# A PEER decoder layer on one core: 170 gathered tokens for 160, and gate pieces of 38 tokens for 32

## The chip, the cores and the metric

The kernel runs on one core of a Trainium2 chip. The metric is the device time of one execution in microseconds (us). The kernel before was run three times, and the median counts. The traces come from the hardware profiler, of one execution each.

## What is computed

The reference is one decoder layer over 512 tokens of width 2048, all in float32: modulation from a conditioning vector, a projection with a short convolution and a differential attention, an output projection, and then the PEER feed-forward part, on which the change works:

```python
def peer_ffn(h, w_q, keys1, keys2, expert_u, expert_v):   # 8 heads, 128 x 128 experts
    ...                                                   # idx, g: (T, 8, 16), the 16 best experts of each head
        u = jnp.take(expert_u, ib, axis=0)
        a = jnp.einsum('thkd,td->thk', u, xb)
        w = (jax.nn.gelu(a.astype(jnp.float32), approximate=False) * gb).astype(xb.dtype)
        vv = jnp.take(expert_v, ib, axis=0)
        return jnp.einsum('thk,thkd->td', w, vv)
```

Each token picks 128 of the 16,384 experts. An expert is a row of `expert_u` and a row of `expert_v`, 2048 floats (8 KB) each.

## The kernel before

The first third of the kernel computes the layer up to the queries of the experts. Then it treats the tokens in two ways, side by side.

**Dense tokens** (`TD = T - TG`, the last 352). All 128 blocks of 128 experts are multiplied with all of these tokens. `u_block(e)` loads block e of `expert_u` (`ur`), turns it on VectorE where it was laid out for that (`u_turn`, `transpose`), and splits it into a high and a low part (`split`: ScalarE makes the high part, VectorE subtracts and writes the low part, both into `ut`). TensorE then does 48 matmuls (16 chunks of the width, three products of high and low parts) with TD columns into `pa`, and ScalarE applies gelu into `ge`. `w_block` multiplies by the gates `g4` and splits the product into `W`. `v_group(ch, dg)` does the same with `expert_v`: for each chunk `ch` of 8 blocks and each quarter `dg` of the width it loads, splits (`vs`) and multiplies, 96 matmuls with TD columns, and VectorE adds the result to `acc`. There are 16 chunks. `ut` and `vs` have two buffers each.

**The gate stage** comes before: for each dense token a 128 x 128 table of gates is made by one matmul of two one-hot tables (`oh` made on VectorE, `og` on GpSimd and ScalarE, eight tokens at a time), and stored to `g_dram` in pieces of `GB` tokens.

**Gathered tokens** (the first `TG` = 160). One token lies on each partition, and an indirect DMA of GpSimd fetches for each partition the row of one of its experts, 1 MB in all (`gathered`, tile `gt`, three buffers). VectorE multiplies it with the token and sums (`gather_u`), and later adds the row of `expert_v` times its weight to `gacc` (`gather_v`). The first 128 tokens take 128 gathers of u and 128 of v. The other 32 tokens form a second group: they lie four times over the partitions (`fold` = 4), each copy taking 32 of a token's 128 experts, so 32 gathers of u and 32 of v. `gather_next` brings the second group's tokens, indices and gates to their places.

`gather_to` spreads these steps evenly over the blocks of the dense part, up to the end of chunk 14. At the end `begin`, `add_gathered` and `store` add everything up for each quarter `dg`: `add_gathered` turns `gacc` on TensorE and sums the copies of the second group on VectorE.

The order of the instructions on each engine is set by a scheduler that works from its own model of times. It keeps the dependences, and each engine then runs its own list strictly in order. So a vector operation that waits for a gather holds up the splits behind it, and TensorE waits for the splits.

Of the kernel before, what the change touches and what calls it, by code (L numbers as in the profile page):

```python
# [15 lines left out]
AF = mybir.ActivationFunctionType  # L16
OP = mybir.AluOpType
# [5 lines left out]
P = 128  # L23
# [8 lines left out]
THETA = 10000.0  # L32
LAM_INIT = 0.8 - 0.6 * math.exp(0.0)

TG = 160
TD = T - TG
CH = 8
AHEAD = 1
GB = 32
GBUF = 3  # L40
LAG = 3
PASSES = ((0, 0), (0, 1), (1, 0))
# [16 lines left out]
OG_ACT = 2  # L59
# [20 lines left out]
def hymba_peer(tc, x, c, positions, w_ada, b_ada, norm1_g, w_in, conv_w, q_norm_g, k_norm_g,  # L80
               lambda_q1, lambda_k1, lambda_q2, lambda_k2, subln_g, w_out, norm2_g,
               w_peer_q, sub_keys1, sub_keys2, expert_u, expert_v, out):
    nc = tc.nc
    x, out = x[0], out[0]
# [14 lines left out]
    with ExitStack() as ctx:  # L99
        const = ctx.enter_context(tc.tile_pool(name="const", bufs=1))  # L100
        y_dram = tc.dram_tile([KC, P, T], F32, name="y_dram")
        x1_dram = tc.dram_tile([KC, P, T], F32, name="x1_dram")
        g_dram = tc.dram_tile([TD // GB, NK, NK, GB], F32, name="g_dram")
        u_dram = tc.dram_tile([NK, P, D], F32, name="u_dram")
        h_dram = tc.dram_tile([TG - P, D], F32, name="h_dram")
        a_dram = tc.dram_tile([P, D], F32, name="a_dram")
# [29 lines left out]
        def px():  # L136
            return psX.tile([P, T], F32, name="px")
# [521 lines left out]
        gate = [(res if i < NG else tk).tile([P, P], F32, name=f"gate{i}", bufs=1) for i in range(NT)]  # L659
# [3 lines left out]
        def dense_tokens(n, behind):  # L663
            k, r = divmod(n, 4)
            q, m = divmod(k, 4)
            t = nc.scalar.activation(hd[4 * m + r][q * 32:(q + 1) * 32],
                                     h2T[k][r * 32:(r + 1) * 32, :, TG:].bitcast(F32), AF.Copy)
            tc.add_manual_dep(t.ins, behind.ins.name, ORDER, reason="work left for the weights")
# [93 lines left out]
        idxu = [None] * NT  # L762
        opT = [None] * NT
        if NG == 2:
            w = P // fold
            ib = res.tile([P, w], U32, name="ib")
            gb_ = res.tile([P, w], F32, name="gb_")

        def finish_select(i):
            gv = gate[i].rearrange("p (h k) -> p h k", k=16)  # L770
# [89 lines left out]
        def w_block(e):  # L860
            if e % 4 == 0:
                G4[0] = up.tile([P, TD // GB, 4, GB], F32, name="g4", bufs=1)
                nc.sync.dma_start(G4[0], g_dram[:, :, e:e + 4, :].rearrange("b p i t -> p b i t"))
            if e % 2 == 0:
                return
            ge = GE.pop(e // 2)
            g_ = ge.rearrange("p i (b t) -> p i b t", t=GB)
            nc.vector.tensor_tensor(out=g_, in0=g_, in1=G4[0][:, :, e % 4 - 1:e % 4 + 1, :].rearrange("p b i t -> p i b t"),
# [42 lines left out]

        def gather_next():
            nc.sync.dma_start(a_dram, gacc)
            w = P // fold
            for f in range(fold):
                nc.sync.dma_start(h2n[f * nb:(f + 1) * nb, :], h_dram)
                nc.sync.dma_start(ib[f * nb:(f + 1) * nb, :], idxu[1][0:nb, f * w:(f + 1) * w])
                nc.sync.dma_start(gb_[f * nb:(f + 1) * nb, :], gate[1][0:nb, f * w:(f + 1) * w])

        steps = []  # L920
        for g in range(NG):
            w = P if g == 0 else P // fold
            if g:
                steps.append((gather_next, ()))
            steps += [(gather_u, (g, j)) for j in range(w)] + [(gather_w, (g, w))] + [(gather_v, (g, j)) for j in range(w)]
# [25 lines left out]
        with tc.tile_pool(name="gs", bufs=2, side="right") as gs:  # L951
            ios = gs.tile([P, P], F32, name="ios", bufs=1)
            nc.gpsimd.iota(ios, pattern=[[1, P]], base=0, channel_multiplier=0, allow_small_or_imprecise_dtypes=True)
            iof = psI.tile([P, P], F32, name="iof")
            nc.scalar.activation(iof, ios, AF.Copy)
            nb_ = TD // GB
            for b in range(nb_):
                gt_ = gs.tile([P, NK, GB], F32, name="gtile")
                for t8 in range(0, GB, 8):
                    i, tt = divmod(TG + b * GB + t8, P)  # L960
                    o = opT[i]
                    oh = gp.tile([P, D], F32, name="gt", bufs=GBUF).rearrange("p (a t n) -> p a t n", a=2, n=P)
                    nc.vector.tensor_tensor(out=oh, in0=iof[:, None, None, :].to_broadcast([P, 2, 8, P]),  # L963
                                            in1=o[:, 0:2, tt:tt + 8, None].to_broadcast([P, 2, 8, P]), op=OP.is_equal)
                    og = gs.tile([P, 8, P], F32, name="og", bufs=OG_BUFS)
                    m = 8 - OG_ACT
                    nc.gpsimd.tensor_tensor(out=og[:, 0:m], in0=oh[:, 0, 0:m],
                                            in1=o[:, 2, tt:tt + m, None].to_broadcast([P, m, P]), op=OP.mult)
                    for j in range(m, 8):
                        nc.scalar.activation(og[:, j], oh[:, 0, j], AF.Copy, scale=o[:, 2, tt + j:tt + j + 1])  # L970
                    for t4 in (4, 0):
                        pg = psV.tile([P, 4, P], F32, name="pv")
                        for j in range(4):
                            gm = nc.tensor.matmul(pg[:, j], oh[:, 1, t4 + j], og[:, t4 + j], start=True, stop=True)  # L974
                        nc.scalar.activation(gt_[:, :, t8 + t4:t8 + t4 + 4], pg.rearrange("p t n -> p n t"), AF.Copy)
                nc.sync.dma_start(g_dram[b], gt_)
                lay_out(min(1 + (b % 8 == 7), len(lay)), gm)
                if b >= nb_ - (RUN - NT):
                    u_block(RUN - nb_ + b, behind=gm if b == nb_ - 1 else None)

# [133 lines left out]
```

## Time and profile before

| what | value |
|---|---|
| time, median of 3 runs | 3346.73 us (3344.19 to 3349.19) |
| the profiled execution: its own time | 3349.88 us |
| its span, first to last instruction | 3347.6 us |
| TensorE busy | 95% of the span |
| VectorE busy | 82% of the span |
| mean granted TensorE clock | 0.978 of 2.4 GHz |

The shares are means over stages with different limits. The profile's time axis starts at the first instruction; the gate stage lies at about 1255 to 1400 us, the dense part with its gathers at 1400 to 3256 us, and the end behind it. In a window's row, an engine's busy time counts operations that overlap once, whereas a group's busy time adds up the durations.

### The profile page before, as it was taken

The numbers are of one execution on the slowest core, as the hardware profiler recorded it, in microseconds if no ns is written. First come the engines' busy times: TensorE is split into PE (matmuls) and PEld (weight loads), VectorE is DVE, ScalarE is ACT, GpSimd is POOL, SyncE is SP. The second block draws the span as 40 slices with busy tenths as digits, with TensorE's granted clock in tenths as the row PEclk, the third lists the DMA queues.
The fourth block names the chain that finished last, engine by engine and source line by source line (L and its number), as shares of the span: only waits on it lengthen the run. The fifth ranks groups of instructions, "written<-read, shape, count | busy, mean of one in ns | idle before, by whom it ended". The sixth has DMA issues, their size and how long they took to land.

```text
span 3347.6 us, 47029 instructions
## 1 busy us (share of the span) xinstructions
PE 3176.0 (95%) x18006; PEld 2945.2 (88%) x18006; DVE 2739.1 (82%) x3631; ACT 1223.3 (37%) x1866; POOL 1057.7 (32%) x709
## 2 busy tenths in 40 slices
PE   5889999999999859999999999999999999999998
PEld 4777877777777659999999999999999999999997
DVE  6888477842338998789999899999999999999975
ACT  5246343343255336632333333333333333333322
POOL 2447333353435634312222232222222222222210
PEclk9999999999999979999999999999999999999998
DMA  9878978966979878989989899998988898999964
GB/s 303 283 257 294 345 250 280 299 211 221 315 256 302 261 243 288 335 290 364 343 332 343 310 333 363 325 338 323 340 333 316 336 354 329 360 330 338 338 222 158
DMA packets 388896, 1017.81 MB, mean 304 GB/s; under 512 B 29713, under 2 KB 108478, under 8 KB 328126
## 3 DMA queue, kind: packets, MB, share of 16 engines
q1 hardware_dynamic: 342590, 679.23, 59.8%
q0 software_dynamic: 46080, 335.56, 25.7%
q8 instruction: 141, 2.31, 0.3%
q14 instruction: 85, 0.70, 0.1%
HBM read 965.11 MB, written 171.18 MB: 339 GB/s over the span
## 4 chain that ended last, share of the span: by engine, by line
PE 55%; DVE 4%; issue 2%; DMA 1%; ACT 0%; POOL 0%; DVEq 0%; ACTq 0%; SPq 0%; POOLq 0%
PE pa L835 26%; PE pv L1004 26%; PE pv L974 2%; DVE gacc L910 1%; DVE ut L90 1%; DMA xs<-x_dram 1%; DVE gt L963 1%; DVE ur L823 1%; DVE vs L90 1%; DMA gt<-in_expert_v_dram,idxu 0%; DMA gt<-in_expert_u_dram,idxu 0%; ACT ut L89 0%; DVE acc L1020 0%; PE pv L1061 0%; DVE gt L897 0%
## 5 line engine op out<-in xcount | busy, mean ns | idle before, releaser
L835 PE MATMUL pa<-hd,ut 128*128 128x352 f32 x6144 | 1067.2, 326 | 37.5 <-DVE ut L90 23.6
L1004 PE MATMUL pv<-W,vs 128*128 128x352 f32 x6144 | 1052.1, 325 | 5.1 <-ACT W L89 2.6
L835 PEld LDWEIGHTS pa<-hd,ut 128*128 128x128 f32 x6144 | 1010.9, 190 | 42.4 <-DVE ut L90 26.6
L1004 PEld LDWEIGHTS pv<-W,vs 128*128 128x128 f32 x6144 | 1001.8, 189 | 8.0 <-ACT W L89 3.5
L90 POOL TENSOR_TENSOR wsp<-wraw,wsp 128x1024 fp32r<-128x1024 f32 x160 | 389.0, 2434 | 557.6 <-ACT wsp L89 525.4
L89 ACT ACTIVATE vs<-vr 128x1024 fp32r<-128x1024 f32 x256 | 271.6, 1061 | 737.9 <-PE pv L1004 687.8
L89 ACT ACTIVATE ut<-ur 128x1024 fp32r<-128x1024 f32 x256 | 269.6, 1056 | 315.2 <-PE pa L835 239.5
L897 DVE SCALAR_TENSOR_TENSOR gt<-gt,h2n 128x2048 f32<-128x2048 f32 x160 | 364.6, 2283 | 18.3 <-DMA gt<-in_expert_u_dram,idxu 18.3
L910 DVE SCALAR_TENSOR_TENSOR gacc<-gt,ga_a,gacc 128x2048 f32<-128x2048 f32 x158 | 369.9, 2341 | 6.8 <-DMA gt<-in_expert_v_dram,idxu 6.7
L889 POOL DMA_INDIRECT gt<-in_expert_u_dram,idxu x128 | 183.0, 1430 | 554.6 <-DVE gt L897 320.8
L90 DVE TENSOR_TENSOR vs<-vr,vs 128x1024 fp32r<-128x1024 f32 x256 | 311.2, 1216 | 57.3 <-ACT vs L89 56.9
L90 DVE TENSOR_TENSOR ut<-ur,ut 128x1024 fp32r<-128x1024 f32 x256 | 310.9, 1219 | 55.6 <-ACT ut L89 54.4
L889 POOL DMA_INDIRECT gt<-in_expert_v_dram,idxu x128 | 172.4, 1347 | 552.3 <-DVE gacc L910 360.1
L89 ACT ACTIVATE wsp<-wraw 128x1024 fp32r<-128x1024 f32 x160 | 169.2, 1058 | 346.5 <-issue 72.0
L507 PE MATMUL pm<-big,wsp 128*128 128x512 f32 x1152 | 285.2, 401 | 0.0
L823 DVE STREAM_TRANSPOSE ur<-ur 128x1024 f32<-128x1024 f32 x232 | 274.5, 1221 | 0.1
L507 PEld LDWEIGHTS pm<-big,wsp 128*128 128x128 f32 x1152 | 214.9, 191 | 42.6
L282 PE MATMUL pqk<-wsp,big 128*128 128x512 f32 x768 | 190.1, 407 | 18.0 <-DVE qk L334 13.6
L748 PE MATMUL pm<-big,wsp 128*128 128x512 f32 x768 | 188.5, 403 | 19.0 <-POOL wsp L90 17.4
L282 PEld LDWEIGHTS pqk<-wsp,big 128*128 128x128 f32 x768 | 148.7, 196 | 53.0 <-DVE qk L334 17.0
L748 PEld LDWEIGHTS pm<-big,wsp 128*128 128x128 f32 x768 | 147.2, 195 | 52.2 <-POOL wsp L90 20.0
L593 PE MATMUL pm<-big,wsp 128*128 128x512 f32 x768 | 182.1, 397 | 6.2 <-DVE x L599 6.2
(274 smaller groups left out, 3024.0 us busy)
## 6 DMA issues: line engine op xcount, KB each, us to landing
ur<-u_dram SPq DMA_DIRECT2D x128, 1024.0 KB, 7.8
vr<-in_expert_v_dram SPq DMA_DIRECT2D x256, 512.0 KB, 7.2
u_dram<-in_expert_u_dram SPq DMA_DIRECT2D x464, 256.0 KB, 6.7
ada_w<-in_w_ada_dram SPq DMA_DIRECT2D x192, 512.0 KB, 5.5
wraw<-in_w_in_dram SPq DMA_DIRECT2D x96, 512.0 KB, 5.7
g_dram<-gtile SPq DMA_DIRECT2D x11, 2048.0 KB, 7.4
g<-g_dram SPq DMA_DIRECT2D x32, 704.0 KB, 9.4
wraw<-in_w_out_dram SPq DMA_DIRECT2D x32, 512.0 KB, 5.5
```

What stands on the lines that cost most here:

```text
L89: hi = nc.scalar.activation(dst[:, 0], src, AF.Copy)
L90: (eng or nc.vector).tensor_tensor(out=dst[:, 1], in0=src, in1=dst[:, 0].bitcast(F32), op=OP.subtract)
L282: nc.tensor.matmul(banks[i], hT[kk][:, a, i * P:(i + 1) * P], ws[:, b, k], start=(kk == last[0] and n == 0), stop=(kk == last[1] and n == 2))
L507: nc.tensor.matmul(banks[n2], ws[:, a, k, n2 * P:(n2 + 1) * P], hT[kk][:, b], start=(kk == 0 and n == 0), stop=(kk == KC - 1 and n == 2))
L593: nc.tensor.matmul(banks[j], ws[:, a, k, j * P:(j + 1) * P], yT[kk0 + k][:, b], start=(kq == 0 and k == 0 and n == 0), stop=(kq == 7 and k ...
L748: nc.tensor.matmul(banks[j], ws[:, a, k, j * P:(j + 1) * P], h2T[kk][:, b], start=(kk == 0 and n == 0), stop=(kk == KC - 1 and n == 2))
L823: nc.vector.transpose(t, t)
L835: mm = nc.tensor.matmul(pa[:, :TD], ut[:, a, j].rearrange("p b r -> p (b r)"), hd[k][:, b], start=(k == 0 and n == 0), stop=(k == KC - 1 a ...
L889: d = nc.gpsimd.indirect_dma_start(out=t, out_offset=None, in_=src, in_offset=bass.IndirectOffsetOnAxis(ap=gidx[g][:, j:j + 1], axis=0))
L897: return lambda: nc.vector.scalar_tensor_tensor(t, t, 1.0, h2n, op0=OP.mult, op1=OP.mult, accum_out=ga_a[:, j:j + 1])
L910: return lambda: nc.vector.scalar_tensor_tensor(gacc, t, a, gacc, op0=OP.mult, op1=OP.add)
L1004: mm = nc.tensor.matmul(pv[j // 2][:, j % 2, :TD], vs[:, a, bb, j * P:(j + 1) * P], W[e0 // 2][:, m, bb], start=(b == 0 and n == 0), stop= ...
```

## The change

`TG` becomes 170, so 342 tokens are dense, and 42 form the second gathered group. They lie three times over the partitions (126 of 128 used), each copy taking up to 43 of a token's 128 experts; the tables of indices and gates are set to zero first, so that what isn't filled adds nothing. The second group so takes 43 gathers of u and 43 of v where it took 32 and 32. `GB` becomes 38, which makes nine pieces of the 342 tokens. A piece is no multiple of eight, so its last step has six tokens, and a step also ends where the table of 128 tokens ends.

```diff
-TG = 160
+TG = 170
...
-GB = 32
+GB = 38
...
-            w = P // fold
+            w = -(-P // fold)
             ib = res.tile([P, w], U32, name="ib")
             gb_ = res.tile([P, w], F32, name="gb_")
+            nc.vector.memset(ib, 0)
+            nc.vector.memset(gb_, 0.0)
...
             nc.sync.dma_start(a_dram, gacc)
-            w = P // fold
+            w = -(-P // fold)
             for f in range(fold):
+                n = min(w, P - f * w)
                 nc.sync.dma_start(h2n[f * nb:(f + 1) * nb, :], h_dram)
-                nc.sync.dma_start(ib[f * nb:(f + 1) * nb, :], idxu[1][0:nb, f * w:(f + 1) * w])
+                nc.sync.dma_start(ib[f * nb:(f + 1) * nb, 0:n], idxu[1][0:nb, f * w:f * w + n])
...
-            w = P if g == 0 else P // fold
+            w = P if g == 0 else -(-P // fold)
...
-                for t8 in range(0, GB, 8):
-                    i, tt = divmod(TG + b * GB + t8, P)
+                pos = 0
+                while pos < GB:
+                    i, tt = divmod(TG + b * GB + pos, P)
+                    n = min(8, GB - pos, P - tt)
...
-                lay_out(min(1 + (b % 8 == 7), len(lay)), gm)
+                lay_out(min(1 + (b % 3 == 2), len(lay)), gm)
```

The scheduler makes a new order. Two places of it follow. The change moves its line numbers by up to eight: L910 is L912, L868 is L870, L1031 is L1039, L1047 is L1055.

The first is VectorE's list around the last split of a block of `expert_u` (the last row with `ut` on the left). `gacc` rows are the uses of gathered rows of `expert_v`, `xs` rows belong to the end of the kernel. Before:

```order
L910 SCALAR_TENSOR_TENSOR gacc<-gt,ga_a,gacc 128x2048
L868 TENSOR_TENSOR ge<-ge,g_27186 128x704
L90 TENSOR_TENSOR ut<-ur,ut 128x1024
L90 TENSOR_TENSOR vs<-vr,vs 128x1024
L90 TENSOR_TENSOR W<-ge,W 128x704
L90 TENSOR_TENSOR ut<-ur,ut 128x1024
L90 TENSOR_TENSOR vs<-vr,vs 128x1024
L90 TENSOR_TENSOR ut<-ur,ut 128x1024
L868 TENSOR_TENSOR ge<-ge,g_27186 128x704
L90 TENSOR_TENSOR W<-ge,W 128x704
L90 TENSOR_TENSOR vs<-vr,vs 128x1024
L1031 SCALAR_TENSOR_TENSOR xs<-acc,modc,xs 128x352 x4
```

Now, from the last split of `ut` on:

```order
L90 TENSOR_TENSOR ut<-ur,ut 128x1024
L912 SCALAR_TENSOR_TENSOR gacc<-gt,ga_a,gacc 128x2048 x2
L90 TENSOR_TENSOR vs<-vr,vs 128x1024
L912 SCALAR_TENSOR_TENSOR gacc<-gt,ga_a,gacc 128x2048
L870 TENSOR_TENSOR ge<-ge,g_27252 128x684
L912 SCALAR_TENSOR_TENSOR gacc<-gt,ga_a,gacc 128x2048
L90 TENSOR_TENSOR W<-ge,W 128x684
L912 SCALAR_TENSOR_TENSOR gacc<-gt,ga_a,gacc 128x2048 x3
L90 TENSOR_TENSOR vs<-vr,vs 128x1024
L1039 SCALAR_TENSOR_TENSOR xs<-acc,modc,xs 128x342 x4
L1020 SCALAR_TENSOR_TENSOR xs<-pv,modc,xs 128x342 x4
L1039 SCALAR_TENSOR_TENSOR xs<-acc,modc,xs 128x342 x4
```

Further down the same list the last uses stand together:

```order
L1039 SCALAR_TENSOR_TENSOR xs<-acc,modc,xs 128x342 x4
L912 SCALAR_TENSOR_TENSOR gacc<-gt,ga_a,gacc 128x2048 x11
L1058 TENSOR_TENSOR ft<-ft,pa 128x42 x4
L1060 SCALAR_TENSOR_TENSOR xs<-ft,modc,xs 128x170 x2
```

Before, the last use of a gathered row stood ahead of the last three splits of `ut`. Now 22 uses stand behind the last split of `ut`, seven ahead of the first `xs` row, four between the rows after it, and eleven in one run.

The second is TensorE's list from the last matmul of the last `expert_u` block on (`pa<-hd,ut`); `pv<-W,vs` are the matmuls with `expert_v`, and `pa<-ident,gacc` turns the finished `gacc`. Now:

```order
L837 MATMUL pa<-hd_7553,ut 128x342 x3
L1012 MATMUL pv<-W,vs 128x342 x39
L1051 MATMUL pa<-ident,ot 128x128 x2
L1012 MATMUL pv<-W,vs 128x342 x81
L1055 MATMUL pa<-ident,gacc 128x128 x2
L1051 MATMUL pa<-ident,ot 128x128 x2
L1069 MATMUL pv<-ident,xs 128x128 x5
L1012 MATMUL pv<-W,vs 128x342 x14
```

Of the 312 matmuls with `expert_v` behind the last `expert_u` block, 120 now stand ahead of the first row that needs the finished `gacc`, and 192 (the quarters 2 and 3) behind it. Before, 323 stood behind the last `expert_u` block, and 49 of them ahead of that row.

## Rows read from the trace of the kernel before

**Rows 1.** The page's first lines: span, busy time of each engine

```profile
span 3347.6 us, 47029 instructions
PE 3176.0 (95%) x18006; PEld 2945.2 (88%) x18006; DVE 2739.1 (82%) x3631; ACT 1223.3 (37%) x1866; POOL 1057.7 (32%) x709
```

**Rows 2.** Windows: each engine's busy time in a stretch, granted clock, DMA share, GB/s

```profile
core 0: us, PE busy (x) PEld busy (x) DVE busy (x) ACT busy (x) POOL busy (x), PEclk, DMA share, GB/s
...
1180.00:1250.00 70.00, 40.38 (x198) 37.88 (x196) 68.92 (x282) 19.82 (x25) 23.39 (x29) 0.76 0.77 243
...
1500.00:3200.00 1700.00, 1691.22 (x10469) 1687.40 (x10468) 1602.47 (x1329) 535.26 (x600) 426.50 (x307) 1.00 0.91 337
...
3250.00:3348.00 98.00, 80.03 (x459) 74.92 (x457) 48.42 (x118) 23.36 (x54) 0.00 (x0) 0.89 0.42 145
```

**Rows 3.** Groups of instructions by line and shape: count, busy us, mean ns

```profile
L835 PE MATMUL pa<-hd,ut 128*128 128x352 f32 x6144 | 1067.2, 326 | 37.5 <-DVE ut L90 23.6 <-ACT ut L89 13.6
L1004 PE MATMUL pv<-W,vs 128*128 128x352 f32 x6144 | 1052.1, 325 | 5.1 <-ACT W L89 2.6 <-DVE vs L90 1.4 <-DVE xs L1012 0.6
...
L910 DVE SCALAR_TENSOR_TENSOR gacc<-gt,ga_a,gacc 128x2048 f32<-128x2048 f32 x158 | 369.9, 2341 | 6.8 <-DMA gt<-in_expert_v_dram,idxu 6.7
...
L90 DVE TENSOR_TENSOR vs<-vr,vs 128x1024 fp32r<-128x1024 f32 x256 | 311.2, 1216 | 57.3 <-ACT vs L89 56.9
...
L507 PE MATMUL pm<-big,wsp 128*128 128x512 f32 x1152 | 285.2, 401 | 0.0
...
L1020 DVE TENSOR_TENSOR acc<-acc,pv 128x704 f32<-128x704 f32 x112 | 96.0, 879 | 4.7 <-PE pv L1004 4.5
```

**Rows 4.** Timeline, stretches of matmuls without a gap: start, length, count

```profile
399.74 1.98 PE L507 MATMUL pm<-big,wsp 128*128 128x512 f32 x8
...
2099.83 2.42 PE L1004 MATMUL pv<-W,vs 128*128 128x352 f32 x14
```

**Rows 5.** The chain that ended last, in the gate stage: start, length, what

```profile
1270.25 3.57 PE pv L974 x32
...
1380.80 1.72 DVE gt L963
1382.99 2.29 DVE gt L963
```

**Rows 6.** Waits from 1500 to 3200 us: total us, times, longest

```profile
DVE vs L90 <- ACT vs L89: 32.8, 28, 2.7
...
DVE ut L90 <- ACT ut L89: 23.0, 23, 2.0
...
DVE gt L897 <- DMA gt<-in_expert_u_dram,idxu: 18.3, 10, 4.4
...
DVE ge L868 <- ACT ge L852: 11.1, 11, 2.3
...
DVE gacc L910 <- DMA gt<-in_expert_v_dram,idxu: 6.7, 2, 3.9
```

**Rows 7.** Timeline of VectorE at one late gather, and the window around it

```profile
1890.40 2.29 DVE L897 SCALAR_TENSOR_TENSOR gt<-gt,h2n 128x2048 f32<-128x2048 f32 x1 [4.39 <-DMA gt<-in_expert_u_dram,idxu]
...
1850.00:1900.00 50.00, 47.03 (x293) 46.73 (x292) 39.91 (x38) 17.23 (x20) 12.86 (x9) 1.00 0.81 292
```

**Rows 8.** Timeline of VectorE and TensorE at the end of the kernel

```profile
3248.16 1.23 DVE L90 TENSOR_TENSOR ut<-ur,ut 128x1024 fp32r<-128x1024 f32 x1 [2.51 <-ACT ut L89]
3256.88 0.89 DVE L868 TENSOR_TENSOR ge<-ge,g 128x704 f32<-128x704 f32 x1 [7.50 <-ACT ge L852]
...
3270.68 2.07 DVE L1031 SCALAR_TENSOR_TENSOR xs<-acc,modc,xs 128x352 f32<-128x352 f32 x4
...
3290.69 6.31 PE L1004 MATMUL pv<-W,vs 128*128 128x352 f32 x24 [0.65 <-DVE xs L1012]
```

**Rows 9.** GpSimd's gather instructions: ns min, median, max; time to landing

```profile
L889 POOL DMA_INDIRECT gt<-in_expert_v_dram,ib x32: 936/1188/3270, 3041.0 to 3221.1; - x32
...
DMA to landing us min/median/max: 5.5/8.5/14.4
```

More of the change, by code (lines that the diff above doesn't have):

```diff
@@ L913, in gather_next @@
             nc.sync.dma_start(a_dram, gacc)
-            w = P // fold
+            w = -(-P // fold)
             for f in range(fold):
+                n = min(w, P - f * w)
                 nc.sync.dma_start(h2n[f * nb:(f + 1) * nb, :], h_dram)
-                nc.sync.dma_start(ib[f * nb:(f + 1) * nb, :], idxu[1][0:nb, f * w:(f + 1) * w])
-                nc.sync.dma_start(gb_[f * nb:(f + 1) * nb, :], gate[1][0:nb, f * w:(f + 1) * w])
+                nc.sync.dma_start(ib[f * nb:(f + 1) * nb, 0:n], idxu[1][0:nb, f * w:f * w + n])
+                nc.sync.dma_start(gb_[f * nb:(f + 1) * nb, 0:n], gate[1][0:nb, f * w:f * w + n])
         steps = []
         for g in range(NG):
-            w = P if g == 0 else P // fold
+            w = P if g == 0 else -(-P // fold)
             if g:
@@ L958, in hymba_peer @@
                 gt_ = gs.tile([P, NK, GB], F32, name="gtile")
-                for t8 in range(0, GB, 8):
-                    i, tt = divmod(TG + b * GB + t8, P)
+                pos = 0
+                while pos < GB:
+                    i, tt = divmod(TG + b * GB + pos, P)
+                    n = min(8, GB - pos, P - tt)
                     o = opT[i]
                     oh = gp.tile([P, D], F32, name="gt", bufs=GBUF).rearrange("p (a t n) -> p a t n", a=2, n=P)
-                    nc.vector.tensor_tensor(out=oh, in0=iof[:, None, None, :].to_broadcast([P, 2, 8, P]),
-                                            in1=o[:, 0:2, tt:tt + 8, None].to_broadcast([P, 2, 8, P]), op=OP.is_equal)
+                    nc.vector.tensor_tensor(out=oh[:, :, 0:n], in0=iof[:, None, None, :].to_broadcast([P, 2, n, P]),
+                                            in1=o[:, 0:2, tt:tt + n, None].to_broadcast([P, 2, n, P]), op=OP.is_equal)
@@ L965, in hymba_peer @@
                     og = gs.tile([P, 8, P], F32, name="og", bufs=OG_BUFS)
-                    m = 8 - OG_ACT
+                    m = max(n - OG_ACT, 1)
                     nc.gpsimd.tensor_tensor(out=og[:, 0:m], in0=oh[:, 0, 0:m],
                                             in1=o[:, 2, tt:tt + m, None].to_broadcast([P, m, P]), op=OP.mult)
-                    for j in range(m, 8):
+                    for j in range(m, n):
                         nc.scalar.activation(og[:, j], oh[:, 0, j], AF.Copy, scale=o[:, 2, tt + j:tt + j + 1])
-                    for t4 in (4, 0):
+                    for t4 in ((4, 0) if n > 4 else (0,)):
+                        c4 = min(4, n - t4)
@@ L972, in hymba_peer @@
                         pg = psV.tile([P, 4, P], F32, name="pv")
-                        for j in range(4):
+                        for j in range(c4):
                             gm = nc.tensor.matmul(pg[:, j], oh[:, 1, t4 + j], og[:, t4 + j], start=True, stop=True)
-                        nc.scalar.activation(gt_[:, :, t8 + t4:t8 + t4 + 4], pg.rearrange("p t n -> p n t"), AF.Copy)
+                        nc.scalar.activation(gt_[:, :, pos + t4:pos + t4 + c4],
+                                             pg[:, 0:c4].rearrange("p t n -> p n t"), AF.Copy)
@@ L976, in hymba_peer @@
+                    pos += n
                 nc.sync.dma_start(g_dram[b], gt_)
-                lay_out(min(1 + (b % 8 == 7), len(lay)), gm)
+                lay_out(min(1 + (b % 3 == 2), len(lay)), gm)
                 if b >= nb_ - (RUN - NT):
```

## The prediction

> **What bounds the kernel now.** I read the shares first [rows 1]: TensorE is busy 95% of the span and VectorE 82%, which as a mean over stages says little. The windows say where it counts [rows 2]: from 1500 to 3200 us, half of the kernel, TensorE is busy 1691.2 of 1700 us at full clock (2.4 GHz, granted 1.00), VectorE 1602.5 (94%), and the DMA engines 91%. So TensorE sets the pace there, with VectorE and DMA just below it. Before the dense part, from 1180 to 1250 us, VectorE sets it (68.9 of 70). After 3250 us none is full: TensorE shows 80.0 of 98 us at a granted clock of 0.89, VectorE 48.4. This end is a chain of loads, splits, matmuls and additions.
>
> VectorE's 97.5 us of idle time in the long stretch are of two kinds [rows 6]. Waits for ScalarE's half of a split or for gelu (32.8, 23.0 and 11.1 us) come about because TensorE hasn't yet freed a buffer; that is spare time. Waits for a gathered row (18.3 and 6.7, together 25.0 us) are not spare: the list is worked off in order, and splits stand behind the gather. One of them shows the price [rows 7]: VectorE waits 4.39 us for a row up to 1890 us, and in this window TensorE loses 3.0 of 50 us.
>
> **What the change does to the dense part.** 12,288 matmuls [rows 3] get 342 columns for 352. Their pitch is from stretches without a gap [rows 4], each with one matmul's duration at its end: 14 of 352 columns take 2.42 us, so with 0.325 for the last [rows 3] the pitch is (2.42 - 0.325) / 13 = 0.161 us. Eight of 512 columns take 1.98, and with 0.401 for the last [rows 3] the pitch is 0.226. The slope is 0.065 / 160 = 0.41 ns a column, so ten columns are worth 4.1 ns. The gate matmuls at 128 columns run at 3.57 / 32 = 0.112 us [rows 5], so no fixed floor per matmul lies near 0.161. Not all 12,288 count: 192 (four blocks of 48) run in the stretch up to 1250 us where VectorE sets the pace, and about 380 come behind the last split of `ut` and belong to the end. The other 11,714 give **-48 us**. Bounds are 0, if something else than columns sets the pitch of 0.161, and -53 if the pitch shrinks in proportion (0.161 x 10 / 352 = 4.6 ns).
>
> The gate stage makes ten tables less, two matmul records of 0.112 us each: **-2 us**. Where VectorE paces its end, one step every 2.2 us [rows 5], ten tokens are worth about the same, and the two extra steps take that back; bounds 0 and -4. Nine stores for eleven carry the same tables. The two memsets, the shorter `hd` copies and the ten more rows of `h_dram` lie in stretches that others pace, and cost nothing as long as they do.
>
> The 22 extra gathers would be 22 x 2.34 = 51 us of VectorE [rows 3] and 22 MB. But the order shows that all 22 of the uses they push out stand behind the last split of `ut`. So the dense part ahead of it holds 320 uses, as many as before. VectorE's work there even falls by some 5 us (220 operations of 0.88 us, 3% shorter [rows 3]), but TensorE's time falls more. In the long stretch the 10,469 matmuls [rows 2] give back 43 us, so 1657 us are left for 1597 us of VectorE. Its idle time goes from 97.5 to 60, and less the 25 us of waits for gathers the spare time goes from 72 to 35. With half the spare time I let TensorE's idle time of 8.8 us there double: **+10 us**. Bounds are 0, since the uses stay as far apart as they were, and +25, all waits for gathers passed on to TensorE. DMA moves the same bytes in 2.5% less time, a share of 0.93 for 0.91.
>
> **What it does to the end.** Before, from the end of the last `ut` split (3249.4) to the end of the span (3347.6), it is 98.2 us [rows 8]. Now VectorE has 22 uses of gathered rows in there, and TensorE can't pass the first turn of `gacc` until the last of them is done; 192 matmuls, half of the last chunk, stand behind it.
>
> First part, up to the last use. VectorE's own work by the order is 22 uses x 2.34 = 51.5, six splits `vs` x 1.22 = 7.3 [rows 3], `ge` and `W` 1.8, and 20 `xs` additions at 2.07 / 4 = 0.52 [rows 8], 10.4: together 71 us. Waits come on top. With three buffers, a row is issued when the use three places ahead is done, so in a run a use can come only every (2.34 + landing) / 3 us. Landing is 5.5 us at least, 8.5 in the median [rows 9]: one use every 2.6 to 3.6 us. In the run of eleven, three rows have landed already; the other eight wait 0.3 to 1.3 us each, 2 to 10 us, and I take 7, nearer the median, as several rows fly at once. The first seven uses need two rounds and a third, 25 us for 19 us of work: +6. That makes 84 us, bounds 71 and 93.
>
> Second part, from there to the end. The same state, half of the last chunk still to multiply, was reached before at 3290.7 [rows 8], 56.9 us from the end. I add 3 us for the additions of quarters 0 and 1, which then were partly done: 60 us, bounds 50 (loads of `xs` that then were waited for lie ready now) and 62.
>
> Together 144 us for 98: **+46 us**, bounds +23 and +57.
>
> A rule that bears on the run of eleven is in the Trainium skill's page "SBUF — State Buffer" (its part on the two sides of the memory): GpSimd and VectorE share a pair of ports that one of them holds for a whole instruction, and a VectorE operation with two inputs in SBUF shuts out a GpSimd one that reads SBUF. The rows would fit: the same gather instruction takes 0.94 to 3.27 us [rows 9], but no row says what ran beside it. By the rule each issue in the run would fall into the next use of a row, and the case is priced as a rival below.
>
> **The sum**, on the profiled execution's own time of 3349.88 us: -48 - 2 + 10 + 46 = +6, so 3355.9. This execution was 3.15 us above the median of 3346.73, so I forecast 3352.7 us, at the edge of what can be told from no change, which I put at 0.2% (6.7 us).
>
> **Rivals.**
> *The end is cheaper, and the kernel faster.* Rows land in 5.5 us with the DMA engines at 42% [rows 2], so the first part takes 74 us, and the second 50: +26. With no new idle time of TensorE the sum is -24, 3323 us. It decides as soon as end and idle time together cost under 43 us. For it: the end is idle on all engines, and transfers can go ahead. Against it: the gathers alone are 1 MB each, and three fly at once. Chance 0.22.
> *VectorE becomes the second bound of the dense part.* Spare time of 35 us is a mean; where the list is denser, every wait for a row reaches TensorE, as in [rows 7]. +25 for +10: 3368 us. For it: 3.0 of 4.39 us got through with twice the spare time. Chance 0.20.
> *The gathers' issue is held up by the uses.* If each of the eight issues takes the 3.27 us of its longest row for the 1.19 of its median, a round is 2.1 us longer, 0.7 a use, and the same in the first seven: 15 x 0.7 = 10. The sum is +16, 3363 us. Against it: in part the median of 8.5 us holds this already. It is the page's rule at work. Chance 0.15.
> *The pitch doesn't follow the columns.* Then 0 for -48 and no new idle time: -2 + 46, 3391 us. The straight line through 352 and 512 speaks against it. Chance 0.05.
>
> The forecast itself, from 3346 to about 3360, has 0.38; most of it lies within 0.2% (0.31), the rest above. So faster 0.22, same 0.31, slower 0.07 + 0.20 + 0.15 + 0.05 = 0.47. The range of eight in ten leaves out most of the last rival, half of the cheap end's lower side and the sum of several bad cases: 3327 to 3377 us.
>
> **What will show it.** In the profile after: matmuls of 342 columns at a pitch of 0.157 us; between 1500 and 3150 us VectorE at about 96%, with TensorE idle for some 18 us; the last `ut` split some 40 us earlier than 3248; from it to the end about 144 us, with eleven uses of `gacc` in a row, TensorE idle for some 30 us ahead of the first turn of `gacc`, and a lower granted clock behind it. The prediction is wrong if TensorE passes the end without that gap, if the last `ut` split is less than 25 us earlier, or if the pitch is still 0.161.

## The result, and the profile after

The change takes 3364.51 us (median of 6 runs, 3361.49 to 3367.57) where the kernel before took 3347.93 beside it (3339.32 to 3350.70). The ratio is 1.0054, with an interval of 1.0041 to 1.0067: slower by 16.6 us, or 0.5%. The forecast was 6 us. The profiled execution took 3364.15 us, with a span of 3362.3.

The first lines of the page of the change, and three of its groups of instructions (count, busy us, mean ns; behind the bar the idle time ahead of them), answer to [rows 1, 3]:

```profile
span 3362.3 us, 47027 instructions
...
PE 3131.3 (93%) x17986; PEld 2899.9 (86%) x17986; DVE 2777.5 (83%) x3652; ACT 1222.3 (36%) x1871; POOL 1096.4 (33%) x733
...
L837 PE MATMUL pa<-hd,ut 128*128 128x342 f32 x6144 | 1044.5, 323 | 35.1 <-DVE ut L90 22.8
L1012 PE MATMUL pv<-W,vs 128*128 128x342 f32 x6144 | 1032.6, 321 | 21.0 <-DVE vs L90 8.6
...
L912 DVE SCALAR_TENSOR_TENSOR gacc<-gt,ga_a,gacc 128x2048 f32<-128x2048 f32 x169 | 396.1, 2344 | 20.3 <-DMA gt<-in_expert_v_dram,ib 17.2
```

TensorE has 45 us less work, and the span is 14.7 us longer all the same. VectorE's uses of a `v` row wait 20.3 us, where they waited 6.8. The windows of the change (the long stretch of [rows 2], and the two parts of the end):

```profile
core 0: us, PE busy (x) PEld busy (x) DVE busy (x) ACT busy (x) POOL busy (x), PEclk, DMA share, GB/s
1500.00:3200.00 1700.00, 1687.36 (x10666) 1682.81 (x10665) 1620.00 (x1357) 542.93 (x611) 435.31 (x308) 1.00 0.92 341
...
3210.00:3305.00 95.00, 33.78 (x178) 31.76 (x177) 69.58 (x51) 8.08 (x10) 30.67 (x20) 0.69 0.79 294
3305.00:3362.00 57.00, 47.31 (x286) 43.90 (x286) 28.41 (x74) 16.06 (x44) 0.00 (x0) 0.89 0.38 130
```

In the long stretch TensorE is still busy for 99% of the time: it is idle for 12.6 us, 8.8 before. In the first part of the end it works for 34 of 95 us. VectorE's timeline names what it waits for there (start, length, in brackets the idle time ahead and its cause):

```profile
1399.08 1.23 DVE L90 TENSOR_TENSOR ut<-ur,ut 128x1024 fp32r<-128x1024 f32 x1 [8.33 <-ACT ut L89]
...
3208.89 1.23 DVE L90 TENSOR_TENSOR ut<-ur,ut 128x1024 fp32r<-128x1024 f32 x1
...
3229.48 2.35 DVE L912 SCALAR_TENSOR_TENSOR gacc<-gt,ga_a,gacc 128x2048 f32<-128x2048 f32 x1 [2.40 <-DMA gt<-in_expert_v_dram,ib]
3233.93 2.35 DVE L912 SCALAR_TENSOR_TENSOR gacc<-gt,ga_a,gacc 128x2048 f32<-128x2048 f32 x1 [2.10 <-DMA gt<-in_expert_v_dram,ib]
...
3245.55 2.03 DVE L1039 SCALAR_TENSOR_TENSOR xs<-acc,modc,xs 128x342 f32<-128x342 f32 x4 [4.07 <-DMA xs<-x_dram]
...
3265.31 2.03 DVE L1039 SCALAR_TENSOR_TENSOR xs<-acc,modc,xs 128x342 f32<-128x342 f32 x4 [2.20 <-DMA xs<-x_dram]
3267.25 7.12 DVE L912 SCALAR_TENSOR_TENSOR gacc<-gt,ga_a,gacc 128x2048 f32<-128x2048 f32 x3
3277.63 2.35 DVE L912 SCALAR_TENSOR_TENSOR gacc<-gt,ga_a,gacc 128x2048 f32<-128x2048 f32 x1 [3.25 <-DMA gt<-in_expert_v_dram,ib]
...
3286.40 2.35 DVE L912 SCALAR_TENSOR_TENSOR gacc<-gt,ga_a,gacc 128x2048 f32<-128x2048 f32 x1 [0.63 <-DMA gt<-in_expert_v_dram,ib]
3291.45 2.35 DVE L912 SCALAR_TENSOR_TENSOR gacc<-gt,ga_a,gacc 128x2048 f32<-128x2048 f32 x1 [2.70 <-DMA gt<-in_expert_v_dram,ib]
...
3302.61 2.35 DVE L912 SCALAR_TENSOR_TENSOR gacc<-gt,ga_a,gacc 128x2048 f32<-128x2048 f32 x1 [2.60 <-DMA gt<-in_expert_v_dram,ib]
```

The last split of `ut` starts 39.3 us earlier than in [rows 8] (6.0 of it because the dense part starts earlier, at 1399.1 for 1405.1), and from its end (3210.1) to the end of the span it is 152.2 us, 98.2 before. Of the 22 uses in there eleven come in a row from 3267.25 to 3304.96; eight of those wait for their row, 11.8 us in all. VectorE's waits for loads from 3210.1 to 3305 us (total us, times, longest):

```profile
DVE gacc L912 <- DMA gt<-in_expert_v_dram,ib: 17.2, 11, 3.3
DVE xs L1039 <- DMA xs<-x_dram: 6.3, 2, 4.1
...
```

TensorE's timeline of the change shows what that costs:

```profile
3237.47 0.66 PE L1012 MATMUL pv<-W,vs 128*128 128x342 f32 x1 [5.61 <-DVE vs L90]
...
3251.04 7.18 PE L1012 MATMUL pv<-W,vs 128*128 128x342 f32 x44 [1.74 <-DVE vs L90]
3305.02 0.69 PE L1055 MATMUL pa<-ident,gacc 128*128 128x128 f32 x2 [46.80 <-DVE gacc L912]
```

It stands still for 46.8 us ahead of the first turn of `gacc`, with half of the last chunk's matmuls behind that turn.

### The profile page after: what moved, and what is told of

Read it like the earlier page. It is cut to its first block, busy times and chain, and to the rows that moved or that the text cites. A ratio compares the mean times of both kernels' runs of the same rounds, so it can differ in the third digit from the quotient of the medians.

```text
span 3362.3 us, 47027 instructions
## 1 busy us (share of the span) xinstructions
PE 3131.3 (93%) x17986; PEld 2899.9 (86%) x17986; DVE 2777.5 (83%) x3652; ACT 1222.3 (36%) x1871; POOL 1096.4 (33%) x733
## 4 chain that ended last, share of the span: by engine, by line
PE 66%; DVE 16%; DMA 11%; issue 4%; POOL 2%; ACT 1%; SPq 1%; DVEq 0%; POOLq 0%; ACTq 0%
PE pa L837 25%; PE pv L1012 25%; PE pm L507 6%; DMA ada_w<-in_w_ada_dram 3%; PE pm L593 3%; PE pv L980 2%; PE pm L282 2%; DVE run L215 2%; PE sp L461 1%; DVE ada_acc L215 1%; DVE gacc L912 1%; DVE tkj L723 1%; DMA u_dram<-in_expert_u_dram 1%; DMA xs<-x_dram 1%; DMA gt<-in_expert_v_dram,ib 1%
## 5 line engine op out<-in xcount | busy, mean ns | idle before, releaser
L837 PE MATMUL pa<-hd,ut 128*128 128x342 f32 x6144 | 1044.5, 323 | 35.1 <-DVE ut L90 22.8
L1012 PE MATMUL pv<-W,vs 128*128 128x342 f32 x6144 | 1032.6, 321 | 21.0 <-DVE vs L90 8.6
L837 PEld LDWEIGHTS pa<-hd,ut 128*128 128x128 f32 x6144 | 990.2, 191 | 39.3 <-DVE ut L90 24.9
L1012 PEld LDWEIGHTS pv<-W,vs 128*128 128x128 f32 x6144 | 982.4, 190 | 26.6 <-DVE vs L90 10.6
L912 DVE SCALAR_TENSOR_TENSOR gacc<-gt,ga_a,gacc 128x2048 f32<-128x2048 f32 x169 | 396.1, 2344 | 20.3 <-DMA gt<-in_expert_v_dram,ib 17.2
L899 DVE SCALAR_TENSOR_TENSOR gt<-gt,h2n 128x2048 f32<-128x2048 f32 x171 | 389.8, 2284 | 4.6 <-DMA gt<-in_expert_u_dram,idxu 4.4
L825 DVE STREAM_TRANSPOSE ur<-ur 128x1024 f32<-128x1024 f32 x232 | 274.9, 1223 | 8.3 <-DMA ur<-u_dram 7.7
L748 PEld LDWEIGHTS pm<-big,wsp 128*128 128x128 f32 x768 | 146.6, 194 | 50.3 <-POOL wsp L90 18.4
```

What stands on the lines that cost most here:

```text
L748: nc.tensor.matmul(banks[j], ws[:, a, k, j * P:(j + 1) * P], h2T[kk][:, b], start=(kk == 0 and n == 0), stop=(kk == KC - 1 and n == 2))
L825: nc.vector.transpose(t, t)
L837: mm = nc.tensor.matmul(pa[:, :TD], ut[:, a, j].rearrange("p b r -> p (b r)"), hd[k][:, b], start=(k == 0 and n == 0), stop=(k == KC - 1 a ...
L899: return lambda: nc.vector.scalar_tensor_tensor(t, t, 1.0, h2n, op0=OP.mult, op1=OP.mult, accum_out=ga_a[:, j:j + 1])
L912: return lambda: nc.vector.scalar_tensor_tensor(gacc, t, a, gacc, op0=OP.mult, op1=OP.add)
L1012: mm = nc.tensor.matmul(pv[j // 2][:, j % 2, :TD], vs[:, a, bb, j * P:(j + 1) * P], W[e0 // 2][:, m, bb], start=(b == 0 and n == 0), stop= ...
```

## The experiments

Theory A: the dense part gives back what ten columns are worth, and the end takes it away, because uses of gathered rows that didn't find a place on VectorE under the matmuls stand between TensorE and the turn of `gacc`. The rivals: the added gathers alone make the price (C), or the shorter dense part alone (D).

For each kernel two numbers are read from VectorE's timeline of its profiled execution. "Dense" runs from the start of the `ut` split at about 1400 us (the first row of the timeline above) to the end of the last one; "end" runs from there to the end of the span.

| kernel | uses behind the last split | dense, us | end, us | ratio to before, interval |
|---|---|---|---|---|
| before | 0 | 1844.3 | 98.2 | |
| the change | 22 | 1811.0 | 152.2 | 1.0054 (1.0041 to 1.0067) |
| e4 gacc added at the very end | 22 | 1809.1 | 128.0 | 0.9994 (0.9983 to 1.0005) |
| e5 columns alone | 13 | 1797.5 | 118.1 | 0.9911 (0.9899 to 0.9924) |
| e6 gathers alone | 20 | 1840.7 | 145.0 | 1.0145 (1.0130 to 1.0159) |
| e7 before, added at the very end | 0 | 1843.1 | 92.6 | 0.9995 (0.9985 to 1.0005) |
| e8 = e4, gates on GpSimd | 31 | 1813.3 | 159.4 | 1.0107 (1.0092 to 1.0121) |
| e9 two parts | 22 | 1809.1 | 124.5 | 0.9984 (0.9974 to 0.9995) |
| e10 before, two parts | 0 | 1846.1 | 95.6 | 1.0006 (0.9995 to 1.0018) |
| e11 rows resident | 22 | 1809.0 | 128.4 | 0.9999 (0.9988 to 1.0011) |
| e12 = e9, lanes by TensorE | 22 | 1808.3 | 123.5 | 0.9968 (0.9957 to 0.9978) |

The change has 22 uses behind the last split; the 26 named in the expectation of e5 was a miscount. How many stand there is fixed by the scheduler's order before the kernel runs.

**e1, e2, e3: an order that spoiled the dense part.** The uses were to be spread evenly by making each split of `ut` follow a use in VectorE's order:

```
+            i = len(uses) - 1 - (23 * (15 - n % 16)) // 16
+            if i >= 0:
+                tc.add_manual_dep(lo.ins, uses[i].ins.name, ORDER, reason="gathered rows in turn")
```

e2 has this order with 342 columns and the 160 + 160 rows of before (each copy of the 42 tokens gathers only 32 of its up to 43 rows, so their last experts are left out), e3 with 352 columns and 171 + 171 rows.

> The changed kernel, with an order-only dependence of each split of ut on a use of a gathered row that was written out a little ahead of it, so that all 342 uses stand ahead of the last split of ut (0 behind it, for 22). Theory A (the loss is the place of the 22 uses: the end is long because TensorE waits there for gacc): the end is again about 98 us from the last split of ut. The dense part now holds 22 more uses, 50 us of VectorE, which makes it about as long as TensorE's part, so its last split of ut comes at 3220 to 3235 us instead of 3209. Together 3318 to 3333 us, faster than both. Theory B (VectorE is the bound and 22 uses cost their 50 us wherever they stand): the last split of ut at about 3255 us, and 3355 to 3365 us, as the changed kernel.

> The changed kernel with the same ordering, but the second group gathers only 32 rows of u and 32 of v for each copy, as before: 320 uses for 342, and the last experts of these 42 tokens are left out of the output. It shows the columns alone. Theory A: the dense part gives back the 39 us that the changed kernel showed, up to 48, and the end is 98 us: 3300 to 3310 us. Theory B (VectorE bounds the dense part already): little of the 48 us comes back, 3325 to 3345 us. If the pitch of a matmul didn't follow its columns, 3345 us.

> 160 gathered tokens and 352 columns in pieces of 32 as before, but the second group of 32 tokens lies only three times over the partitions, so that it takes 43 and 43 gathers as in the change (342 uses), with the ordering that keeps all uses ahead of the last split of ut. Theory A: VectorE has 60 to 70 us of idle time to spare in the dense part at 352 columns, so 50 us more of it cost 5 to 20 us: 3353 to 3368 us. Theory B: they cost their 50 us, 3390 to 3400 us.

Measured: 3581.25 us (1.0715), 3545.25 us (1.0606) and 3595.71 us (1.0755). No theory had that. Of e1, first its window over the long stretch, then TensorE's waits over the whole span and VectorE's from 1500 to 3200 us (total us, times, longest):

```profile
1500.00:3200.00 1700.00, 1529.88 (x9228) 1499.74 (x9227) 1460.41 (x1212) 475.33 (x531) 392.41 (x285) 0.96 0.83 307
```

```profile
PE pa L842 <- DVE ut L829: 150.3, 66, 11.8
...
```

```profile
...
DVE ur L825 <- DMA ur<-u_dram: 42.5, 21, 8.3
DVE gacc L917 <- DMA gt<-in_expert_v_dram,idxu: 36.4, 26, 4.6
DVE gt L904 <- DMA gt<-in_expert_u_dram,idxu: 35.0, 24, 3.1
...
DVE gt L904 <- DMA gt<-in_expert_u_dram,ib: 13.0, 8, 2.6
```

TensorE is idle for 170 of 1700 us and waits 150.3 us for splits of `ut`, 22.8 in the change. VectorE is less busy too (1460 for 1620 us): it waits 84.4 us for gathered rows (36.4, 35.0 and 13.0) and 42.5 us for loads of `u`. That agrees with [rows 7], where a split behind a late use held up TensorE in one place; how much of the price comes from the rows and how much from the loads of `u` isn't taken apart. One part of theory A held: with no use behind the last split, the end is short again, 94.4 us in e1, 94.6 in e2 and 94.2 in e3. The order's own price hides what e2 and e3 were to tell, so they were made again without it (e5, e6).

**e4: the gathered part behind the last v matmul.**

```
-ADD_AT = ((0,), (1,), (2,), (3,))
-STORE_AT = ((), (0,), (1,), (2, 3))
+ADD_AT = ((), (), (), (0, 1, 2, 3))
+STORE_AT = ((), (), (), (0, 1, 2, 3))
```

> The changed kernel, with the additions of the gathered tokens and the stores of all four quarters written behind the last group of matmuls with expert_v, not one after each quarter. The scheduler still puts 22 uses behind the last split of ut, but all 312 matmuls with expert_v now stand ahead of the first turn of gacc, and the splits of vs between the uses. Theory A: TensorE no longer idles for 47 us ahead of gacc; the uses and the 12 splits are done at about 3310 us as now, and behind them only four quarters of turns, additions and stores are left, some 25 to 30 us instead of 57: 3335 to 3345 us. If the wait of TensorE for gacc were not what makes the end long, the time stays at 3364.

Measured: 3341.25 us. TensorE's timeline of e4:

```profile
3294.81 9.20 PE L1012 MATMUL pv<-W,vs 128*128 128x342 f32 x44 [0.77 <-DVE vs L90]
3314.91 0.69 PE L1055 MATMUL pa<-ident,gacc 128*128 128x128 f32 x2 [10.90 <-DVE gacc L912]
```

The wait falls from 46.8 to 10.9 us, the end by 24.2, and the ratio by 0.6%, with the same 22 uses behind the last split. So the wait of TensorE, not the uses as such, holds that part of the price.

**e7: the same edit in the kernel before.**

> The kernel before the change with the gathered part added and the output stored behind the last v matmul, as in e4. gacc is ready there before TensorE comes to it, so nothing is to be saved. Theory A: the additions and stores lose the matmuls that they stood under; in e4 the stretch from gacc to the end has 30 us, in the kernel before 13 us lie behind the last v matmul, so 3352 to 3365 us, and e4's gain is net of about as much. Rival (the place of the additions is worth something by itself, whatever the wait): 3325 to 3340 us.

Measured: 3340.99 us, no change clear of the noise (0.9985 to 1.0005). The loss that theory A named didn't come, and the rival's gain neither. Where no use is late, the place of the additions is worth little: the end of the one profiled execution is 5.6 us shorter, which the interval would cover too. So most of the 24.2 us that e4 takes from the end is the change's wait.

**e5 and e6: each half of the change alone.** e5 is the change, but each of the three copies of the 42 tokens gathers only 32 of its up to 43 rows, so that the last experts of these tokens are left out; e6 has `TG = 160`, `GB = 32` and `fold = 3`.

> 170 tokens leave the dense part (342 columns, gates in nine pieces), but only 160 + 160 rows are gathered, as before the change: the last experts of the 42 tokens of the second group are left out. Nothing else is added, unlike in e2. 13 uses of gathered rows stand behind the last split of u (26 in the change, none before). Theory A (the end's price is that of uses that VectorE can't take under the matmuls, whether because there are more of them or because there is less time): dense part 41 to 48 us shorter, end 20 to 30 us longer for half as many uses behind, 3315 to 3335 us. Rival C (the price comes from the added gathers alone): the end keeps its 98 us, 3295 to 3310 us.

> 352 columns and 160 tokens as before the change, but the second group lies three times over the partitions, so 171 + 171 rows are gathered (the output is that of the reference). 20 uses stand behind the last split of u. Theory A: no gain in the dense part, VectorE has 22 uses of 2.3 us more, the end is 25 to 45 us longer, 3368 to 3390 us. Rival D (the 22 uses find VectorE's gaps, and the price comes from the shorter dense part alone): 3344 to 3355 us.

Measured: 3315.35 us (0.9911) and 3391.94 us (1.0145). C and D fall. Theory A's ranges are met at their edges: e5's end grows by 19.9 us (20 to 30 expected), and e6's by 46.8 (25 to 45), so that e6 takes 2 us more than its range. Of e5 the long stretch, the last split, and TensorE's wait:

```profile
1500.00:3200.00 1700.00, 1696.42 (x10755) 1695.30 (x10755) 1604.29 (x1344) 549.31 (x616) 432.78 (x299) 1.00 0.91 335
```

```profile
3201.68 1.23 DVE L90 TENSOR_TENSOR ut<-ur,ut 128x1024 fp32r<-128x1024 f32 x1 [0.64 <-ACT ut L89]
```

```profile
PE pa L1055 <- DVE gacc L912: 13.2, 1, 13.2
```

Of e6 the same two:

```profile
3242.71 1.23 DVE L90 TENSOR_TENSOR ut<-ur,ut 128x1024 fp32r<-128x1024 f32 x1 [0.75 <-PE pv L1012]
```

```profile
PE pa L1055 <- DVE gacc L912: 39.9, 1, 39.9
```

The columns alone take 46.8 us from the dense part, and the order puts 13 uses behind the last split although none was added: the end grows by 19.9 us. The gathers alone leave the dense part nearly as it was (-3.6 us) and add 46.8 us to the end. The two ratios multiply to 0.9911 x 1.0145 = 1.0055, and the change has 1.0054 (each is known to some 0.0013), so the halves add up in the total. In the parts they don't. The dense part is 33.3 us shorter in the change, where the halves have 50.4 together, and the end 54.0 us longer, where they have 66.7. The halves put 33 uses behind the last split between them and the change 22: e5's dense part holds 307 uses, the change's 320. So the change has 11 more of them under its matmuls, which fits a longer dense part and a shorter end.

**e8: gates on GpSimd.** In e4, `nc.vector.tensor_tensor` of the gates became `nc.gpsimd.tensor_tensor`.

> e4 with the multiplication of the gates in the dense part on GpSimd instead of VectorE: 64 instructions of 0.86 us leave VectorE, 55 us. Theory A (VectorE's time under the matmuls sets how late the last use is): the last use ends 10 us or more earlier against the last split of u, 3325 to 3338 us. Rival (GpSimd's own work delays the gathers, or VectorE slows down beside it): 3345 to 3380 us.

Measured: 3378.13 us (1.0107), the rival's time. GpSimd's waits and VectorE's for gathered rows from 1500 to 3180 us, and the window from the last split of `ut` to the end of the last use:

```profile
...
POOL ge L870 <- ACT ge L854: 87.9, 26, 7.2
...
POOL ge L870 <- issue: 50.3, 17, 8.3
```

```profile
...
DVE gacc L912 <- DMA gt<-in_expert_v_dram,idxu: 6.2, 5, 3.2
...
DVE gt L899 <- DMA gt<-in_expert_u_dram,idxu: 3.1, 4, 1.3
```

```profile
3213.30:3343.11 129.81, 63.57 (x371) 60.04 (x369) 103.31 (x77) 14.28 (x16) 44.57 (x29) 0.79 0.83 307
```

GpSimd works its list in order, and its multiplication stands 138 us at the head of it (87.9 us for the gelu, 50.3 with no cause shown). But few rows come late by that in the long stretch: VectorE waits 9.3 us for them, 4.0 in e4, and the dense part is only 4.2 us longer. The loss is in the end, 159.4 us for 128.0, where the scheduler's order has 31 uses for 22. VectorE is busy there for 103.3 us, 81.9 in e4, and waits 21.6 us for rows, 11.4 in e4. So 55 us less for VectorE didn't bring the uses under the matmuls. Why the scheduler put them so late isn't shown.

**e11: the last rows resident.**

```
-            t = gathered(expert_v, g, j)
+            t = h2n if (g, j) > (1, 16) else gathered(expert_v, g, j)
```

> The change, but the last 26 uses read a row that lies in SBUF already instead of the gathered one; the 26 gathers are left out, and the output isn't the reference's for the 42 tokens. The order on VectorE is nearly the same, with eleven uses in a row at the end. Theory A' (of the first part's 11 us above the forecast, the waits for rows, 17.2 us in all, are the cause): last use some 15 us earlier against the last split of u, TensorE's wait for gacc 30 to 38 us, 3345 to 3353 us. Rival (VectorE's own work and the loads of x set it, and the waits for rows are covered): 3358 to 3366 us.

Here 26 uses, the 22 behind the last split among them, read a row that lies in SBUF, and their gathers are left out.

Measured: 3343.45 us (0.9999), just below what theory A' gave. VectorE's and TensorE's timelines of e11, and the window between the last split and the turn of `gacc`:

```profile
3211.96 1.23 DVE L90 TENSOR_TENSOR ut<-ur,ut 128x1024 fp32r<-128x1024 f32 x1
...
3259.56 26.23 DVE L912 SCALAR_TENSOR_TENSOR gacc<-h2n,ga_a,gacc 128x2048 f32<-128x2048 f32 x11
```

```profile
3285.84 0.69 PE L1055 MATMUL pa<-ident,gacc 128*128 128x128 f32 x2 [32.04 <-DVE gacc L912]
```

```profile
3213.20:3285.80 72.60, 32.93 (x177) 31.55 (x176) 69.16 (x50) 8.04 (x10) 0.00 (x0) 0.74 0.28 94
```

With the same uses in nearly the same order, the first part takes 72.6 us (3213.2 to 3285.8) for 94.9. VectorE is busy for 69.2 of it, as in the change (69.6 of 95), so the waits that come with the gathers are 22.3 us: 17.2 for rows and 5.1 of the 6.3 for `xs`.

**e9, e10 and e12: what the last uses really hold up.** In e9 the first group's 128 tokens are added in each quarter's turn and the tiles 0, 2 and 3 are stored a quarter later; only the second group's 42 tokens, tile 1 and what the last quarter still has follow the last v matmul:

```
+                    add_first(dg)
+                    if dg:
+                        store(dg - 1, (0, 2, 3))
+                    if dg == 3:
+                        store(3, (0, 2, 3))
+                        for f in range(4):
+                            add_second(f)
+                        for f in range(4):
+                            store(f, (1,))
```

e10 is the same in the kernel before. e12 adds up the three lanes of e9 in one matmul, with a 128x42 matrix `lanes` of ones and zeros, where a copy and two additions did it:

```
+                nc.tensor.matmul(pt[:, j % 2 * P:j % 2 * P + nb], gacc[:, k * P:(k + 1) * P], lanes, start=True, stop=True)
```

> The change, with the gathered part added in two steps: the first group's 128 tokens in each quarter's turn, with the stores of the token tiles 0, 2 and 3 a quarter later; the second group's 42 tokens, which alone need the last uses, behind the last v matmul, with the stores of tile 1 (the output is that of the reference). 22 uses stand behind the last split of u. Theory A (what is lost in the end is work held up by the wait for the last use): as in e4 the v matmuls don't wait, and in the 30 us from gacc to the end only half of the additions and a quarter of the stores are left, 14 to 20 us: 3325 to 3337 us, faster than e4 and than the kernel before. Rival (the uses at the end are the limit, and VectorE's earlier additions push them out by what is saved): 3338 to 3348 us.

> The same two steps in the kernel before the change (160 tokens; the output is that of the reference). No use stands behind the last split of u, and nothing waited for gacc. Theory A: little to gain, 3337 to 3348 us. Rival (the order of additions and stores is better by itself): 3320 to 3335 us, and then e9 has to be held against this time.

> e9, with the three lanes of the second group's 42 tokens added up by TensorE: gacc's 128 columns times a 128x42 matrix of ones and zeros, so a copy of ScalarE and two additions of VectorE fall away for each of 16 pieces. In e9 the stretch behind the last use has 16.6 us, in which TensorE waits after each pair of pieces. Theory A (this stretch is a chain of small steps, each waiting for the one before): 10 to 13 us are left, 3330 to 3335 us. Rival (the stores and their landing set it): 3336 to 3339 us as e9.

Measured: e9 3337.36 us, between theory A's range and the rival's, e10 3345.31 and e12 3333.20 us, both in theory A's range of time. TensorE's timeline of e9, and of e12:

```profile
3308.52 0.92 PE L1072 MATMUL pv<-ident,xs 128*128 128x128 f32 x4 [0.23 <-DVE xs L1020]
3322.34 0.69 PE L1058 MATMUL pa<-ident,gacc 128*128 128x128 f32 x2 [12.90 <-DVE gacc L912]
```

```profile
3325.47 1.66 PE L1063 MATMUL pa<-lanes,gacc 128*128 128x42 f32 x6 [12.99 <-DVE gacc L916]
```

Behind the last use 16.6 us are left in e9 (30.5 in e4), but that use ends 107.9 us after the last split of `ut`, 97.5 in e4. So of 14 us saved, 10 were paid ahead of it, as the rival had it: from the last split to the last use VectorE is busy for 88.2 us in e9 and 81.9 in e4, and 3.8 us of its waits in e9 stand ahead of copies for the earlier stores. e10 shows no gain in the kernel before. e12 has 14.2 us behind the last use, 2.4 less than e9 but more than the 10 to 13 expected, and its time is 4 us lower; the two intervals still overlap. e12 is faster than both kernels: by 0.3% (0.2 to 0.4) than before.

## Why the forecast was right in the mechanism, and 11 us short

The time lies within the range. The sum had the right parts, signs and places, but the forecast lay within 0.2% of the time before, and 0.5% slower came out. Slower had 0.47 of the chances, 0.40 of it by way of rivals. Point by point:

- **Columns, -48 us.** Nearly right. In e5, where VectorE leaves TensorE alone, 10,755 matmuls take 1696.4 us, 0.1577 us each; before it is 1691.2 / 10,469 = 0.1615 [rows 2]. So ten columns gave 3.8 ns for 4.1, and 11,714 times that is 45 us. e5's dense part is 46.8 us shorter, some 5 of it less idle time in the long stretch. "The pitch doesn't follow the columns" is out.
- **Gate stage, -2 us.** Not to be seen above the spread. The first `ut` split comes 6 us earlier in the change's profiled execution, but in the seven kernels of the table with 342 columns it starts at 1404.3 us in the mean (1399.1 to 1408.3) and in the four with 352 columns at 1404.7.
- **TensorE's idle time doubled, +10.** The long stretch shows 12.6 us idle for 8.8, where 18 was forecast, and VectorE at 95.3% for 96. But e5 has 3.6 there, and its pitch is 0.1577 for 0.1582 in the change. So against the columns alone the change loses 13.5 us in its dense part, which holds 13 more uses than e5's. In all the dense part is 33.3 us shorter (35 in e4, e9 and e11); the forecast was 38.
- **22 uses behind the last split.** Right as a count, but the reason was half of it: I put them all down to the extra gathers. In e5 the order puts 13 out with a shorter dense part and no gather added.
- **First part of the end, 84 us.** This is the term of the sum that was mis-sized: 94.9 us. VectorE's own work was right (71 us forecast, 69.6 measured). Of waits 13 us were in the sum. Uses waited 17.2 us for rows, 5.4 ahead of the run of eleven (6 forecast) and 11.8 in it (7 taken, with 10 as the bound). And the two `xs` additions waited 6.3 us for their load, which the sum didn't have, though such waits stand in the end of the kernel before as well. SyncE's timeline of the change has the issue of these two loads:

```profile
3225.84 0.47 SPq L1035 DMA_DIRECT2D xs<-x_dram  x1
...
3251.43 0.46 SPq L1035 DMA_DIRECT2D xs<-x_dram  x1
```

  The additions start 19.7 and 13.9 us after that (at 3245.55 and 3265.31); in the kernel before the same two start 10.1 and 7.9 us after their issue (3260.56 and 3278.45), in e11 12.1 and 7.4. So the loads land later beside the gathers, and not because they are issued late; which part of the transfer is slower stays open.
- **Second part, 60 us.** 57.3 us, 55.8 in e11.
- **The end in all, +46.** +54.0, within the bound of 57. TensorE's wait ahead of the first turn, put at some 30 us, is 46.8; 10.9 of the difference is the longer first part. Dense part and end together are 20.7 us longer in the profiled execution, for 8 forecast; the start that is 6 us earlier takes part of it back, which is chance by the starts under "Gate stage", and the medians show 16.6.

Of the rivals, the cheaper end had rows that land soon (74 us) and a second part of 50. e11, where the last rows lie ready, shows 72.6 and 55.8, so even then the end costs 30.2 us more than before, for that rival's 26. e4, e9 and e12 come to 25 to 30 by another way, a TensorE that waits less. VectorE as the second bound of the dense part is seen in e1 alone, where the order made it so.

The rival of the gathers' issue gave 3363 us, which is close by chance, for its mechanism shows but is smaller than its 10 us. GpSimd's timeline of the change in the run of eleven:

```profile
3270.36 2.44 POOL L891 DMA_INDIRECT gt<-in_expert_v_dram,ib  x1 [8.14 <-DVE gacc L912]
3273.10 2.08 POOL L891 DMA_INDIRECT gt<-in_expert_v_dram,ib  x1 [0.30 <-issue]
3275.49 0.94 POOL L891 DMA_INDIRECT gt<-in_expert_v_dram,ib  x1 [0.30 <-issue]
3280.74 0.94 POOL L891 DMA_INDIRECT gt<-in_expert_v_dram,ib  x1 [4.31 <-DVE gacc L912]
3283.97 2.61 POOL L891 DMA_INDIRECT gt<-in_expert_v_dram,ib  x1 [2.30 <-DMA gt<-in_expert_v_dram,ib]
3286.89 2.68 POOL L891 DMA_INDIRECT gt<-in_expert_v_dram,ib  x1 [0.30 <-issue]
3289.87 0.94 POOL L891 DMA_INDIRECT gt<-in_expert_v_dram,ib  x1 [0.30 <-issue]
3294.56 2.95 POOL L891 DMA_INDIRECT gt<-in_expert_v_dram,ib  x1 [3.75 <-DVE gacc L912]
```

The issues at 3275.49 and 3289.87 fall into gaps of VectorE (idle from 3274.4 to 3277.6 and from 3288.8 to 3291.5) and take 0.94 us; those at 3273.10 and 3286.89 start while a use runs, and end 0.8 us after it (at 3275.18 for 3274.37, and at 3289.57 for 3288.75). It is the same outside the end: from 2000 to 3300 us, 71 issues that start beside a split of `ut` (two inputs) end 0.81 us after it in the median, and 23 that start beside a turn of `ur` (L825, one input) take 0.94. Five of eight in the run are long, 2.08 to 2.95 us, together 8.1 us over 0.94 each. That agrees with the rule cited in the prediction (the Trainium skill's page "SBUF — State Buffer", section "Who interferes with whom": a VectorE operation with two SBUF inputs and a GpSimd operation that reads SBUF shut each other out). But with three buffers in flight a lengthened issue costs a third of its length, so my estimate is 3 us of the 22, worked out from these rows. The rows show the issue and the operation beside it, and no run here takes its price apart from the landing itself.

## What to carry to other kernels

Before work is moved from one engine to another, ask which of the two still has time where the first is the bound: here ten tokens freed 45 us of TensorE and cost 22 uses x 2.34 = 51 us of VectorE, which was already 94% busy, and the scheduler's order put 22 uses in the end, where nothing covers them. It puts uses there also when only the cover shrinks (e5). Whether VectorE could have taken them under the matmuls in a better order isn't shown: the one order tried for it (e1) brought waits of its own. And where a tail can't be avoided, put in front of it everything that does not need it, at the place where the engine that works in order meets it: that was worth 0.6% in e4, 0.7% in e9 and 0.9% in e12 (which adds up the lanes on TensorE besides), and nothing clear of the noise in the kernel without a tail (e7, e10).

## What was not expected

- The halves of the change multiply to its ratio (e5, e6), although their dense parts and their ends don't add up to those of the change. That the ratios agree to 0.0001 is chance, since each is known to some 0.0013.
- Uses behind the last split seem to cost little at first and more later: 13 of them lengthen the end by 19.9 us (1.5 us each), 20 by 46.8 (2.3), 22 by 54.0 (2.5). These are three kernels with different columns and orders, so it is a hint and no law.
- The lower clock that the prediction looked for behind TensorE's wait isn't there in the mean: 0.89 is granted in the second part, as in the end of the kernel before (0.89 from 3250 us on, [rows 2]), and the second part takes 57.3 us, for 56.9 before. Only its first 10 us show 0.70. The window of the wait has 0.69, a mix of the levels of 1.2 and 2.4 GHz.
- Edges in the order of VectorE's list, with no new wait on a semaphore, cost over 200 us (e1).
